# A token mixer's output product on Trainium2, rewritten from eight block products into seven products of quarters

## The chip, the cores and the metric

The kernel runs on one core of one Trainium2 chip. The metric is device time in microseconds (us) of one execution. The kernel before took 2018.16, 2018.16 and 2019.1 us in three runs: the median is 2018.16 us.

## What is computed

A decoder trunk of two layers over 512 tokens of width 1024, in float32. Each layer is a SwiGLU half-step, a token mixer and a second SwiGLU half-step, with a LayerNorm after each:

```python
x = layer_norm(ALPHA * x + 0.5 * swiglu(x, ffn1_w13[l], ffn1_w2[l]), ln_g[l, 0], ln_b[l, 0])
m = mixer(x, w_in[l], ..., w_branch_a[l], w_branch_b[l], w_out[l])
x = layer_norm(ALPHA * x + m, ln_g[l, 1], ln_b[l, 1])
x = layer_norm(ALPHA * x + 0.5 * swiglu(x, ffn2_w13[l], ffn2_w2[l]), ln_g[l, 2], ln_b[l, 2])
```

The end of the mixer is what matters here:

```python
y_a = o @ w_branch_a                                  # heads of the recurrence, 512 x 512
y_b = (u * mixed.reshape(B, T, SG_WIDTH)) @ w_branch_b
y = jax.nn.sigmoid(za) * y_a + jax.nn.sigmoid(zb) * y_b    # 512 tokens x 1024
return y @ w_out                                      # 1024 x 1024
```

## The kernel before, in words

**Products.** A float32 operand is split into two fp32r parts, hi and lo: `split` (L126 on ScalarE copies the source into hi, L127 on VectorE writes source minus hi into lo). One product is then three matmuls (hi hi, hi lo, lo hi) that add up in PSUM. Weights come over SyncE's queue into a ring of four raw buffers (`raw`, NRAW = 4), and their parts go to a ring of ten (`w`, NW = 10). The eight PSUM banks go round as one ring too.

**Seven products.** Most products of the kernel are made with seven products of quarter matrices in the place of eight, with sums and differences of quarters as operands (the table P1 to P7). The class `Seven` does this for the second products of the SwiGLUs, 11 pairs of 128-wide blocks each. Its method `sums_in_dram` forms the weight sums t1 to t4 with copying and accumulating DMAs on GpSimd's (POOL's) queue, in DRAM, long ahead of use. `activation_sums` forms s1 and s2 on VectorE (s3, s4 take the place of quarters of the activations) and splits s1 and s2; `later` splits the rest. `two_b`, `two_c` and `two_d` load and split the weights. `run` issues the products: P1, P6, P5 into the banks pA, pB, pC, then P2 and P3 into pA and pC, which end token rows 0 and 1 (128 tokens each), then P7 into pB and P4 into pF, which end rows 2 and 3. `add_to` (L202) adds a bank of 128 x 512 into the rows of the residual stream x on VectorE. `norm` works off the LayerNorm of a row: nm on VectorE (L215), the squares on ScalarE (L218), rstd on GpSimd (L186, L187), two steps in place on VectorE (L229, L230); its rows are then handed to a side task, `to_features`.

**The end of the mixer.** For each of eight 128-wide column blocks d of y, two projections of 12 matmuls each (`proj`, L155) make the branches' part, VectorE multiplies them by the gates z and adds the two (L1338, L1340), and the sum is split into yt. Two neighbouring blocks d, d + 1 share a load of the branch weights. `out_proj` then takes the product with w_out as eight blocks: the first three blocks k for all four token rows, the others row by row, so that the rows end one after the other, each followed by its norm. Weight loads, splits and matmuls stand in the order in which the code writes them, on each engine. The only things set in by time are the side tasks of `Flow`: a generator waits until an estimated clock (216 ns for a matmul) has passed its due time, then takes a step at one of the ticks that follow each group of three matmuls. So `to_features`, started by the norm with a delay, puts the transposes of a row (L176), and the splits of the transposed x (xh, xl; four tiles of 256 features, two token rows to each half) between the matmuls around it.

**Beyond it.** `first_weights` is called within the output product: it loads and splits the weights a and b of the next SwiGLU's first two blocks. That SwiGLU begins with them on the first 256 tokens (pa, pb; L155; 256-wide matmuls), which need the transposed rows 0 and 1, and later the other 256 tokens; then follow its pairs of blocks with seven products (fX, fA, fC; L661). Other pieces of the mixer that the prediction names: the recurrence's heads, whose outputs need rs, worked out by GpSimd (L186, L187), and `ln_params` (L192, L193), which loads the LayerNorm's factors over GpSimd's queue.

## Time and profile before

| | |
|---|---|
| runs | 2018.16, 2018.16, 2019.1 us; median 2018.16 |
| the profiled execution | 2016.08 us, of which its span (first to last instruction) 2014.3 |
| TensorE (PE) busy | 2003.1 us, 99% of the span, 13600 matmul records |
| TensorE's weight load (PEld) | 1863.7 us, 93% |
| VectorE (DVE) | 1659.4 us, 82% |
| ScalarE (ACT) | 1055.2 us, 52% |
| GpSimd (POOL) | 364.6 us, 18% |
| HBM | read 401.35 MB, written 147.85 MB: 273 GB/s over the span |

The profile follows one execution; its engines' names stand above in brackets, SP is SyncE, whose only work here is to issue DMAs. A row of a view names a line of the kernel, the engine, the operation, the tiles (out<-in) with their shape, and its times; "x4" are four instructions in one row. In a row of a timeline the first number is the start from the span's start and the second the time that the row lasted. "[1.36 <-ACT sq L218]" says that the engine stood idle 1.36 us before it, released by that instruction. A name ending in q ("POOLq", "SPq") is an engine's queue of DMAs; the last number of such a row is the median time from issue to landing.

### The profile page before, as it was taken

The numbers are of one execution on the slowest core, as the hardware profiler recorded it, in microseconds if no ns is written. First come the engines' busy times: TensorE is split into PE (matmuls) and PEld (weight loads), VectorE is DVE, ScalarE is ACT, GpSimd is POOL, SyncE is SP. The second block draws the span as 40 slices with busy tenths as digits, with TensorE's granted clock in tenths as the row PEclk, the third lists the DMA queues.
The fourth block names the chain that finished last, engine by engine and source line by source line (L and its number), as shares of the span: only waits on it lengthen the run. The fifth ranks groups of instructions, "written<-read, shape, count | busy, mean of one in ns | idle before, by whom it ended". The sixth has DMA issues, their size and how long they took to land.

```text
span 2014.3 us, 34802 instructions
## 1 busy us (share of the span) xinstructions
PE 2003.1 (99%) x13600; PEld 1863.7 (93%) x13600; DVE 1659.4 (82%) x2443; ACT 1055.2 (52%) x1545; POOL 364.6 (18%) x493
## 2 busy tenths in 40 slices
PE   9999999999999999999999999999999999999998
PEld 8999988998998999998899999888989989999986
DVE  8888888977766798889789889889778657988986
ACT  5545665336543455556555456652465435454563
POOL 0322002311000133210122320032110001332101
PEclk9999999999999999999999999999999999999999
DMA  6999776885343289987649997778853533999773
GB/s 240 271 266 235 250 261 225 198 228 185 102 169 115 105 231 264 255 229 265 207 148 284 266 244 261 250 235 208 211 164 96 180 112 110 259 257 243 247 252 125
DMA packets 173060, 425.67 MB, mean 211 GB/s; under 512 B 19264, under 2 KB 19392, under 8 KB 172896
## 3 DMA queue, kind: packets, MB, share of 16 engines
q1 hardware_dynamic: 114624, 265.41, 38.9%
q0 software_dynamic: 58272, 158.04, 32.5%
q8 instruction: 107, 1.75, 0.3%
q14 instruction: 57, 0.47, 0.1%
HBM read 401.35 MB, written 147.85 MB: 273 GB/s over the span
## 4 chain that ended last, share of the span: by engine, by line
PE 99%; DVE 0%; issue 0%; ACT 0%; DVEq 0%; ACTq 0%
PE fX L661 22%; PE fC L661 11%; PE pA L414 6%; PE pB L414 6%; PE pC L414 6%; PE cX L992 6%; PE fA L661 6%; PE y L290 4%; PE y L155 4%; PE pF L414 3%; PE cC L992 3%; PE f L155 2%; PE q L155 2%; PE iX L414 2%; PE g L155 2%; PE pa L155 2%
## 5 line engine op out<-in xcount | busy, mean ns | idle before, releaser
L126 ACT ACTIVATE h_pa<-ra 128x1024 fp32r<-128x1024 f32 x80 | 84.5, 1056 | 191.3 <-DVE ra L641 185.3
L355 POOL DMA_DIRECT2D t<-in_w_dram x176 | 145.8, 905 | 207.8 <-DMA t<-in_w_dram 115.6
L127 DVE TENSOR_TENSOR l_pc<-rc,h_pc 128x1024 fp32r<-128x1024 f32 x80 | 97.8, 1222 | 49.6 <-ACT h_pc L126 49.6
L355 POOL DMA_DIRECT2D t<-t x104 | 56.8, 547 | 287.8 <-DMA t<-in_w_dram 260.0
L127 DVE TENSOR_TENSOR l_pa<-ra,h_pa 128x1024 fp32r<-128x1024 f32 x80 | 97.7, 1222 | 2.5 <-ACT h_pa L126 2.4
L127 DVE TENSOR_TENSOR l_b<-r_b,h_b 128x1024 fp32r<-128x1024 f32 (+1 forms) x61 | 73.4, 1204 | 23.0 <-ACT h_b L126 22.3
L186 POOL TENSOR_SCALAR rstd<-ssq 128x1 f32<-128x1 f32 x23 | 18.5, 806 | 398.7 <-ACT sq L218 398.7
L661 PE MATMUL fX<-xh,l_pa 128*128 128x256 f32 x320 | 90.6, 283 | 0.0
L661 PE MATMUL fA<-xh,h_pc 128*128 128x256 f32 x320 | 90.6, 283 | 0.0
L661 PE MATMUL fA<-xl,h_pc 128*128 128x256 f32 x320 | 90.6, 283 | 0.0
L661 PE MATMUL fA<-xh,l_pc 128*128 128x256 f32 x320 | 90.6, 283 | 0.0
L661 PE MATMUL fC<-xs1h,h_pt 128*128 128x256 f32 x320 | 90.6, 283 | 0.0
L661 PE MATMUL fC<-xs1l,h_pt 128*128 128x256 f32 x320 | 90.6, 283 | 0.0
L661 PE MATMUL fC<-xs1h,l_pt 128*128 128x256 f32 x320 | 90.6, 283 | 0.0
L661 PE MATMUL fX<-xs2h,h_pa 128*128 128x256 f32 x320 | 90.6, 283 | 0.0
L661 PE MATMUL fX<-xs2l,h_pa 128*128 128x256 f32 x320 | 90.6, 283 | 0.0
L661 PE MATMUL fX<-xs2h,l_pa 128*128 128x256 f32 x320 | 90.6, 283 | 0.0
L661 PE MATMUL fC<-xs4h,h_pd 128*128 128x256 f32 x320 | 90.6, 283 | 0.0
L661 PE MATMUL fC<-xs4l,h_pd 128*128 128x256 f32 x320 | 90.6, 283 | 0.0
L661 PE MATMUL fC<-xs4h,l_pd 128*128 128x256 f32 x320 | 90.6, 283 | 0.0
L661 PE MATMUL fX<-xs3h,h_pb 128*128 128x256 f32 x320 | 90.6, 283 | 0.0
L661 PE MATMUL fX<-xs3l,h_pb 128*128 128x256 f32 x320 | 90.6, 283 | 0.0
(488 smaller groups left out, 7919.1 us busy)
## 6 DMA issues: line engine op xcount, KB each, us to landing
t<-in_w_dram POOLq DMA_DIRECT2D x88, 512.0 KB, 9.9
t<-t POOLq DMA_DIRECT2D x104, 256.0 KB, 4.8
t<-in_w_dram POOLq DMA_DIRECT2D x88, 256.0 KB, 7.1
r_c<-in_w_dram SPq DMA_DIRECT2D x44, 512.0 KB, 4.7
r_d<-t SPq DMA_DIRECT2D x88, 256.0 KB, 4.0
ra<-in_w_dram SPq DMA_DIRECT2D x80, 256.0 KB, 6.1
rb<-in_w_dram SPq DMA_DIRECT2D x80, 256.0 KB, 8.0
rc<-in_w_dram SPq DMA_DIRECT2D x80, 256.0 KB, 8.4
```

The costliest lines, as they stand in the source:

```text
L126: pin(S.activation(hi, src, AF.Copy))
L127: pin(V.tensor_tensor(lo, src, hi.bitcast(F32), op=ALU.subtract))
L155: PE.matmul(ps[:, n0:n0 + n], a[:, cs], m[:, n0:n0 + n], start=(i == 0), stop=(i == 3 * nk - 1))
L186: G.tensor_scalar(r, ssq, inv, eps, op0=ALU.mult, op1=ALU.add)
L290: PE.matmul(ys[t][q], a[:, ts], m[:, q * 512:(q + 1) * 512], start=(k == 0 and i == 0), stop=(k == nk - 1 and i == 2))
L355: tc.keep_in_program_order(nc.gpsimd.dma_start(*of(k), **kw))
L414: PE.matmul(ps[tt], a[:, ts], m, start=(start and k == self.order[0] and z == 0), stop=(stop and k == self.order[-1] and z == 2), skip_gro ...
L661: PE.matmul(ps[:, half[z]], a[:, ms], v, start=start, stop=(m == 3 and i == 2), skip_group_check=not (first and z == 0))
L992: PE.matmul(ps[:, half[z]], a[:, ms], v, start=first and z == 0 and m == 0 and i == 0, stop=(m == 3 and i == 2), skip_group_check=not (fir ...
```

## The change

The mixer's product with w_out goes through `Seven` in place of `out_proj`, which is gone. K is 8 blocks, so there are four pairs (k, k + 4); `run` and `sums_in_dram` get the few branches that so short a product wants (`few`, `early_d`). Each mixer makes its own weight sums with 24 DMAs on GpSimd's queue: a side task, started after the v projections, issues four at a time, 12000 ns of the estimated clock apart. The y blocks are made in the order of the pairs, d and d + 4 after one another, straight into the room of the quarters, and the activation sums of the pair follow at once. The arrays of the weights w_br and w_out are laid out anew by the host ahead of the run. In `run`, the steps `later(left.pop(0), 0)` and `later(k, 2)` change places, for the SwiGLUs too.

```diff
@@ -276,41 +276,6 @@
...
-    def out_proj(nk, lhs, w_of, c, ln, tag, first_weights):
...
-        tail = NW // 2
-        for k in range(nk):
-            w[k] = weights(w_of(k), f"{tag}{k}")
-            if k < nk - tail:
-                for t in range(NT):
-                    unit(k, t, (0, 1))
-        g, b = ln_params(*ln)
-        xs = load_rows()
-        begin_features()
-        for t in range(NT):
-            if t == 2:
-                first = first_weights()
-            sums = small("sums", 2)
-            for q in range(2):
-                for k in range(nk - tail, nk):
-                    unit(k, t, (q,))
-                add_to(xs[t], q, c, ys[t][q], sums)
-            norm(t, xs[t], sums, g, b, False, 9500.0)
-        return first
@@ -330,16 +295,16 @@
...
-        def __init__(self, w_of, order, spilled):
+        def __init__(self, w_of, order, spilled, tag="t"):
...
-        def sums_in_dram(self, pairs, group=3):
+        def sums_in_dram(self, pairs, group=3, gap=SUM_GAP):
@@ -353,7 +318,7 @@
                     for of, kw in ((copy, {}), (add, {"accum_op": ALU.add})):
                         for k in ks:
                             tc.keep_in_program_order(nc.gpsimd.dma_start(*of(k), **kw))
-                        yield 0.0, SUM_GAP
+                        yield 0.0, gap
         def part(self, k, a):
@@ -460,6 +425,7 @@
             A, B, C = ([bank(f"{v}{tt}") for tt in range(2)] for v in ("pA", "pB", "pC"))
+            few = self.n < NH2
             tail = 2
             fetched = {}
             left = list(ks)
@@ -475,14 +441,17 @@
                     fetched[v] = self.fetched(v)
                 h1, l1, h2, l2 = fetched[k]
                 ops["A11", k], ops["s1", k], ops["s2", k] = (h1, l1), (h2[:, 0], l2[:, 0]), (h2[:, 1], l2[:, 1])
-                if i < NH2 - tail:
+                if i < self.n - tail:
                     for ps, p in ((A, P1), (B, P6), (C, P5)):
                         for tt in range(2):
                             mm(ps, p, [k], tt, True, True)
-                if i >= LATER:
+                if few:
+                    if i:
+                        later(left.pop(0), 0)
+                elif i >= LATER:
                     for _ in range(min(2, len(left) - LATEST)):
                         later(left.pop(0), 0)
-                if i == LATER:
+                if i == (0 if few else LATER):
                     xs = load_rows()
             u = wk.tile([P, 2, 512], F32, tag="rs", name="u", bufs=2)
             for ps, p in ((A, P1), (B, P6), (C, P5)):
@@ -498,18 +467,20 @@
             tail = 2
             for i, k in enumerate(ks):
                 self.two_c(k)
-                if i < NH2 - LATEST:
+                if left and (few or i in (2, 3, 6)):
+                    later(left.pop(0), 0)
+                if few or i < NH2 - LATEST:
                     later(k, 2)
-                if left and i in (2, 3, 6):
-                    later(left.pop(0), 0)
-                if i in (4, 5):
-                    add_to(xs[i - 4], 1, -c, B[i - 4])
-                if 0 < i < NH2 - tail:
+                at = i - (1 if few else 4)
+                if at in (0, 1):
+                    add_to(xs[at], 1, -c, B[at])
+                if 0 < i < self.n - tail:
                     for ps, p in ((A, P2), (C, P3)):
                         for tt in range(2):
                             mm(ps, p, ks[0:2] if i == 1 else [k], tt, False, True)
             g, b = ln_params(*ln)
-            for k in ks[0:4]:
+            early_d = 2 if few else 4
+            for k in ks[0:early_d]:
                 self.two_d(k, True)
             if not last:
                 begin_features()
@@ -523,11 +494,11 @@
             F = [bank(f"pF{tt}") for tt in range(2)]
             tail = NW // 2
             for i, k in enumerate(ks):
-                if i in range(1, LATEST + 1):
+                if not few and i in range(1, LATEST + 1):
                     later(ks[i - LATEST - 1], 2)
-                if i >= 4:
+                if i >= early_d:
                     self.two_d(k)
-                if i < NH2 - tail:
+                if i < self.n - tail:
                     for ps, p in ((B, P7), (F, P4)):
                         for tt in range(2):
                             mm(ps, p, [k], tt, ps is F, True)
@@ -1274,6 +1245,8 @@
         flow.finish(in_dram)
         two_tokens()
         late.append(flow.add(all_out(), 4000.0))
+        so = Seven(lambda k: w_out[l, k], list(range(KT // 2)), [], "o")
+        out_sums = flow.add(so.sums_in_dram(so.order, 4, 12000.0), 8000.0)
         moments = []
         for t in range(NT):
             v = vt[t // 2][:, t % 2, :]
@@ -1324,24 +1297,23 @@
         s.clear()
         for t in late:
             flow.finish(t)
-        ys = []
         wbr = [None, None]
-        for d in range(KT):
-            yt = slot(f"yt{d}", F32R)
-            zs = []
-            for br, src in enumerate((ogs, sg)):
-                if d % 2 == 0:
-                    wbr[br] = weights(w_br[l, br, d // 2], f"br{br}{d}")
-                ps = bank(f"y{br}{d}")
-                proj(ps, wbr[br], (d % 2) * 512, lambda k: (src[k][:, 0, :], src[k][:, 1, :]), NH)
-                zv = z[br][d // 2][:, d % 2, :]
-                V.tensor_tensor(zv, zv, ps, op=ALU.mult)
-                zs.append(zv)
-            V.tensor_tensor(zs[0], zs[0], zs[1], op=ALU.add)
-            split(yt[:, 0, :], yt[:, 1, :], zs[0])
-            ys.append(yt)
-        return out_proj(KT, lambda k: (ys[k][:, 0, :], ys[k][:, 1, :]), lambda k: w_out[l, k], 1.0 / ALPHA, (l, 1),
-                        "wo", next_weights)
+        for k in range(4):
+            for a in range(2):
+                d = k + 4 * a
+                zs = []
+                for br, src in enumerate((ogs, sg)):
+                    if a == 0:
+                        wbr[br] = weights(w_br[l, br, k], f"br{br}{k}")
+                    ps = bank(f"y{br}{d}")
+                    proj(ps, wbr[br], a * 512, lambda h: (src[h][:, 0, :], src[h][:, 1, :]), NH)
+                    zv = z[br][d // 2][:, d % 2, :]
+                    V.tensor_tensor(zv, zv, ps, op=ALU.mult)
+                    zs.append(zv.rearrange("p (h t) -> p h t", h=2))
+                V.tensor_tensor(so.part(k, a), zs[0], zs[1], op=ALU.add)
+            so.activation_sums(k)
+        flow.finish(out_sums)
+        return so.run(1.0 / ALPHA, (l, 1), False, [], next_weights)
     lb = const.tile([P, DEPTH, NH], F32, name="lb")
     om = const.tile([P, DEPTH, NH], F32, name="om")
@@ -1455,12 +1427,12 @@
...
-    br = np.stack([np.asarray(v) for v in (w_branch_a, w_branch_b)], 1).reshape(DEPTH, 2, NH, P, 4, 2, P)
+    br = np.stack([np.asarray(v) for v in (w_branch_a, w_branch_b)], 1).reshape(DEPTH, 2, NH, P, 2, 4, P)
...
-        "w_br": c(br.transpose(0, 1, 4, 3, 5, 2, 6)).reshape(DEPTH, 2, 4, P, D),
-        "w_out": c(w_out).reshape(DEPTH, KT, P, D), "ln_g": c(ln_g), "ln_b": c(ln_b),
+        "w_br": c(br.transpose(0, 1, 5, 3, 4, 2, 6)).reshape(DEPTH, 2, 4, P, D),
+        "w_out": quarters(np.asarray(w_out), KT // 2), "ln_g": c(ln_g), "ln_b": c(ln_b),
```

VectorE's order, layer 0, at the end of the output product and around the hand-over to the SwiGLU. Names: y20 and y21 are the banks of the two halves of row 2, x1 and x2 rows of the stream, tr00 and tr01 hold the transposed row 0, tr10 and tr11 row 1, xh and xl are their parts. Before:

```order
L230 SCALAR_TENSOR_TENSOR x1_6851<-x1_6851,rstd_6954,lnb_6846 128x512 x2
L127 TENSOR_TENSOR xl0_6858<-tr00_7003,xh0_6857 128x2x128
L202 SCALAR_TENSOR_TENSOR x2_6853,sums_6987<-y20_6721,x2_6853 128x512
L127 TENSOR_TENSOR xl1_6860<-tr00_7003,xh1_6859 128x2x128
L127 TENSOR_TENSOR xl2_6862<-tr01_7018,xh2_6861 128x2x128
L202 SCALAR_TENSOR_TENSOR x2_6853,sums_6987<-y21_6722,x2_6853 128x512
L127 TENSOR_TENSOR xl3_6864<-tr01_7018,xh3_6863 128x2x128
L215 TENSOR_SCALAR nm_7042<-sums_6987 128x1
L229 SCALAR_TENSOR_TENSOR x2_6853<-x2_6853,nm_7042,lng_6845 128x512 x2
L230 SCALAR_TENSOR_TENSOR x2_6853<-x2_6853,rstd_7047,lnb_6846 128x512 x2
L127 TENSOR_TENSOR xl0_6858<-tr10_7069,xh0_6857 128x2x128
L127 TENSOR_TENSOR xl2_6862<-tr11_7083,xh2_6861 128x2x128
```

After, from the end of row 1's norm; a21 and b21 are weights of the SwiGLU's block 21, the second that it takes, pB0, pF0 the banks of row 2 and pB1, pF1 those of row 3:

```order
L230 SCALAR_TENSOR_TENSOR x1_6812<-x1_6812,rstd_7061,lnb_6981 128x512 x2
L127 TENSOR_TENSOR l_a21_7101<-r_a21_7098,h_a21_7100 128x1024
L127 TENSOR_TENSOR l_b21_7107<-r_b21_7104,h_b21_7106 128x1024
L202 SCALAR_TENSOR_TENSOR x2_6814,sums_7012<-pB0_6775,x2_6814 128x512
L202 SCALAR_TENSOR_TENSOR x2_6814<-pB0_6775,x2_6814 128x512
L202 SCALAR_TENSOR_TENSOR x3_6816,sums_7013<-pB1_6776,x3_6816 128x512
L202 SCALAR_TENSOR_TENSOR x2_6814,sums_7012<-pF0_7070,x2_6814 128x512
L202 SCALAR_TENSOR_TENSOR x3_6816<-pB1_6776,x3_6816 128x512
L215 TENSOR_SCALAR nm_7137<-sums_7012 128x1
L127 TENSOR_TENSOR xl0_6999<-tr00_7171,xh0_6998 128x2x128
L202 SCALAR_TENSOR_TENSOR x3_6816,sums_7013<-pF1_7071,x3_6816 128x512
L127 TENSOR_TENSOR xl0_6999<-tr10_7246,xh0_6998 128x2x128
```

Before, the splits of the transposed rows 0 and 1 stood among the additions and norms of the rows behind them: xl0 of row 0 right behind the norm of row 1, xl0 of row 1 (from tr10) right behind that of row 2. Now the norm's last step of row 1 is followed by two weight splits, all additions of rows 2 and 3 and the start of row 2's norm, with xl0 of row 0 behind nm and xl0 of row 1 behind the last addition of row 3.

TensorE's order at the same place: the output product's end, and the first matmuls of the SwiGLU (pa10 and pb10, the two parts of block 10, the first that it takes). Before:

```order
L290 MATMUL y31_6724<-h_wo7_6841,yt7_6685 128x512
L290 MATMUL y31_6724<-l_wo7_6842,yt7_6685 128x512
L290 MATMUL y31_6724<-h_wo7_6841,yt7_6685 128x512
L155 MATMUL pa10_7153<-xh0_6857,h_a10_6965 128x256
L155 MATMUL pa10_7153<-xl0_6858,h_a10_6965 128x256
L155 MATMUL pa10_7153<-xh0_6857,l_a10_6966 128x256
L155 MATMUL pa10_7153<-xh0_6857,h_a10_6965 128x256
L155 MATMUL pa10_7153<-xl0_6858,h_a10_6965 128x256
```

After:

```order
L176 MATMUL tr01_7185<-ident_67,x0_6810 128x128 x4
L379 MATMUL pF1_7071<-h_d3_7082,s33_6977 128x512
L379 MATMUL pF1_7071<-l_d3_7083,s33_6977 128x512
L379 MATMUL pF1_7071<-h_d3_7082,s33_6977 128x512
L176 MATMUL tr10_7246<-ident_67,x1_6812 128x128 x4
L176 MATMUL tr11_7257<-ident_67,x1_6812 128x128 x4
L155 MATMUL pa10_7242<-xh0_6998,h_a10_7088 128x256
L155 MATMUL pb10_7243<-xh0_6998,h_b10_7094 128x256
L155 MATMUL pa10_7242<-xl0_6999,h_a10_7088 128x256
L155 MATMUL pa10_7242<-xh0_6998,l_a10_7089 128x256
L155 MATMUL pa10_7242<-xh0_6998,h_a10_7088 128x256
L155 MATMUL pa10_7242<-xl0_6999,h_a10_7088 128x256
```

Before, the pa matmuls began behind the last y with the transposes of rows 0 and 1 done long ago, and ran on to 21 of them before the transposes of row 2. Now the transposes tr01 and tr10, tr11 stand among and right behind the last three matmuls of pF1, and pa and pb alternate behind them.

GpSimd's order in layer 0, where the heads' rs are formed. Before, only these stood here, and the LayerNorm's factors (lng) came next:

```order
L186 TENSOR_SCALAR rs_5878<-ms_5876 128x4
L187 TENSOR_TENSOR rs_5878<-rs_5878,mhalf_68 128x4
L186 TENSOR_SCALAR rs_5896<-ms_5894 128x4
L187 TENSOR_TENSOR rs_5896<-rs_5896,mhalf_68 128x4
L192 DMA lng_6845<-in_ln_g_dram 128x1024
```

After (o13, o2 and o4 are the sums in DRAM):

```order
L320 DMA o130_5257<-in_w_out_dram 256x1x512
L320 DMA o131_5258<-in_w_out_dram 256x1x512
L320 DMA o132_5259<-in_w_out_dram 256x1x512
L320 DMA o133_5260<-in_w_out_dram 256x1x512
L320 DMA o20_5261<-o130_5257 128x512
L320 DMA o20_5261<-o131_5258 128x512
L320 DMA o22_5262<-o132_5259 128x512
L320 DMA o22_5262<-o133_5260 128x512
L186 TENSOR_SCALAR rs_5900<-ms_5898 128x4
L187 TENSOR_TENSOR rs_5900<-rs_5900,mhalf_68 128x4
L186 TENSOR_SCALAR rs_5918<-ms_5916 128x4
L187 TENSOR_TENSOR rs_5918<-rs_5918,mhalf_68 128x4
```

Four accumulating and four copying DMAs stand ahead of these rs, and eight further DMAs behind them.

More of the change, by code (lines that the diff above doesn't have):

```diff
@@ L277, in need @@
                 ready[t] = None
-    def out_proj(nk, lhs, w_of, c, ln, tag, first_weights):
-        ys = [[bank(f"y{t}{q}") for q in range(2)] for t in range(NT)]
-        w = {}
-        def unit(k, t, qs):
-            hi, lo = w[k]
-            lh, ll = lhs(k)
-            ts = slice(t * P, (t + 1) * P)
-            for i, (a, m) in enumerate(((lh, hi), (lh, lo), (ll, hi))):
-                for q in qs:
-                    PE.matmul(ys[t][q], a[:, ts], m[:, q * 512:(q + 1) * 512],
-                              start=(k == 0 and i == 0), stop=(k == nk - 1 and i == 2))
-            flow.tick(3 * MM * len(qs))
-        tail = NW // 2
-        for k in range(nk):
-            w[k] = weights(w_of(k), f"{tag}{k}")
-            if k < nk - tail:
-                for t in range(NT):
-                    unit(k, t, (0, 1))
-        g, b = ln_params(*ln)
-        xs = load_rows()
-        begin_features()
-        for t in range(NT):
-            if t == 2:
-                first = first_weights()
-            sums = small("sums", 2)
-            for q in range(2):
-                for k in range(nk - tail, nk):
-                    unit(k, t, (q,))
-                add_to(xs[t], q, c, ys[t][q], sums)
-            norm(t, xs[t], sums, g, b, False, 9500.0)
-        return first
     def load_rows():
@@ L337, in __init__ @@
             self.r, self.t, self.last = {}, {}, None
-            self.t13 = [dram.tile([P, 2, 512], F32, name=f"t13{k}", tag=f"t13{k}", bufs=1) for k in range(n)]
-            self.t2 = [dram.tile([P, 2, 512], F32, name=f"t2{k}", tag=f"t2{k}", bufs=1) for k in range(0, n, 2)]
-            self.t4 = [dram.tile([P, 512], F32, name=f"t4{k}", tag=f"t4{k}", bufs=1) for k in range(n)]
-        def sums_in_dram(self, pairs, group=3):
+            self.t13 = [dram.tile([P, 2, 512], F32, name=f"{tag}13{k}", tag=f"{tag}13{k}", bufs=1) for k in range(n)]
+            self.t2 = [dram.tile([P, 2, 512], F32, name=f"{tag}2{k}", tag=f"{tag}2{k}", bufs=1) for k in range(0, n, 2)]
+            self.t4 = [dram.tile([P, 512], F32, name=f"{tag}4{k}", tag=f"{tag}4{k}", bufs=1) for k in range(n)]
+        def sums_in_dram(self, pairs, group=3, gap=SUM_GAP):
             for at in range(0, len(pairs), group):
```

## Prediction

> **What bounds the kernel now.** I read the page first: busy times, then the chain that ended last.
>
> ```profile
> span 2014.3 us, 34802 instructions
> PE 2003.1 (99%) x13600; PEld 1863.7 (93%) x13600; DVE 1659.4 (82%) x2443; ACT 1055.2 (52%) x1545; POOL 364.6 (18%) x493
> PE 99%; DVE 0%; issue 0%; ACT 0%; DVEq 0%; ACTq 0%
> ```
>
> The span is TensorE's own work. Nothing else is late anywhere, so a matmul taken away is worth its whole time, unless what was hidden beside it comes out. I therefore cut the windows view at the edges of the stage that changes, in layer 0: the output product (627 to 672.5), then the second SwiGLU's first blocks up to its first product of pairs (697.5).
>
> ```profile
> 627.30:640.00 12.70, 12.70 (x57) 10.52 (x57) 6.42 (x7) 5.83 (x6) 0.00 (x0) 1.00 0.52 165
> 640.00:660.00 20.00, 20.00 (x90) 16.54 (x90) 11.16 (x20) 5.56 (x7) 2.53 (x4) 1.00 0.33 107
> 660.00:672.50 12.50, 12.50 (x65) 10.40 (x64) 8.83 (x20) 4.85 (x13) 4.18 (x6) 1.00 0.15 51
> 672.50:685.00 12.50, 12.50 (x106) 12.46 (x105) 6.76 (x16) 6.15 (x18) 2.52 (x4) 1.00 0.93 327
> 685.00:697.50 12.50, 12.50 (x107) 12.50 (x106) 11.77 (x19) 9.12 (x16) 0.00 (x0) 1.00 0.01 2
> ```
>
> Columns: window, its length, then busy time of PE, PEld, DVE, ACT, POOL, granted clock, DMA share, GB/s. PE fills every window; VectorE (DVE) has 26.4 of 45.2 us in the product and 44.9 of 70.2 in all. So VectorE has 25 us to spare in this stretch, and any gain must live within them. TensorE's timeline gives the fixed points.
>
> ```profile
> 627.34 0.62 PE L290 MATMUL y<-h_wo,yt 128*128 128x512 f32 x2
> 628.25 1.07 PE L290 MATMUL y<-h_wo,yt 128*128 128x512 f32 x4
> 629.61 1.07 PE L290 MATMUL y<-h_wo,yt 128*128 128x512 f32 x4
> 672.70 0.28 PE L155 MATMUL pa<-xh,h_a 128*128 128x256 f32 x1
> 672.82 0.28 PE L155 MATMUL pa<-xl,h_a 128*128 128x256 f32 x1
> 675.25 0.60 PE L176 MATMUL tr<-ident,x 128*128 128x128 f32 x4
> 697.50 0.28 PE L661 MATMUL fX<-xh,h_pa 128*128 128x256 f32 x1
> ```
>
> Six 512-wide matmuls start between 628.25 and 629.61: 0.2267 us each; a 256-wide one takes 0.12. I count time from the product's first matmul: T = 627.34. The SwiGLU's first matmul stands at T+45.36, its products at T+70.16.
>
> **The change part by part.** *Matmuls.* 8 x 4 x 2 x 3 = 192 become 7 products x 4 x 2 x 3 = 168 of the same shape: 24 x 0.2267 = 5.44 us less per mixer, 10.9 in two. TensorE could be at the SwiGLU at T+39.9.
>
> *VectorE.* The quarters need 14 weight splits of 1024 columns where 8 served (six more), sums and splits of the activations, six more additions into the rows, two into pB. All stand in one in-order queue. Durations come from the same code at the end of the first SwiGLU, and from the norm of this stage:
>
> ```profile
> 301.00 1.89 DVE L127 TENSOR_TENSOR s<-r,s 128x512 fp32r<-128x512 f32 x3
> 302.80 2.35 DVE L127 TENSOR_TENSOR l_d<-r_d,h_d 128x1024 fp32r<-128x1024 f32 x2
> 305.07 0.68 DVE L202 SCALAR_TENSOR_TENSOR x<-pA,x 128x512 f32<-128x512 f32 x1
> 305.68 0.69 DVE L202 SCALAR_TENSOR_TENSOR x<-pC,x 128x512 f32<-128x512 f32 x1
> 309.91 1.41 DVE L229 SCALAR_TENSOR_TENSOR x<-x,nm,lng 128x512 f32<-128x512 f32 x2
> 311.24 1.41 DVE L230 SCALAR_TENSOR_TENSOR x<-x,rstd,lnb 128x512 f32<-128x512 f32 x2
> ...
> 662.94 0.42 DVE L127 TENSOR_TENSOR xl<-tr,xh 128x256 fp32r<-128x256 f32 x1
> 663.28 0.68 DVE L202 SCALAR_TENSOR_TENSOR x<-y,x 128x512 f32<-128x512 f32 x1
> 674.40 0.21 DVE L215 TENSOR_SCALAR nm<-sums 128x1 f32<-128x1 f32 x1
> 675.97 1.42 DVE L229 SCALAR_TENSOR_TENSOR x<-x,nm,lng 128x512 f32<-128x512 f32 x2 [1.36 <-ACT sq L218]
> 677.85 1.42 DVE L230 SCALAR_TENSOR_TENSOR x<-x,rstd,lnb 128x512 f32<-128x512 f32 x2 [0.46 <-POOL rstd L187]
> 679.19 0.75 DVE L127 TENSOR_TENSOR xl<-tr,xh 128x256 fp32r<-128x256 f32 x2
> ```
>
> From start to start: 1.135 us for 1024 columns, 0.605 for 512, 0.665 for one half of a norm's step, 0.34 for 256; a norm takes 4.8 us from nm to its end. Now the order of the changed kernel. The SwiGLU's first matmul with xl0 needs xl0 of token rows 0 and 1, and the second of these splits stands on VectorE behind everything that the product asks for. From T up to it there are 27 rows of 512, 14 of 1024, 8 norm halves, 6 of 256 and three nm: 16.3 + 15.9 + 5.3 + 2.0 + 0.5 = 40.0 us, without one pause.
>
> Pauses there will be. For them I need ScalarE's split and the loads:
>
> ```profile
> 632.53 1.06 ACT L126 ACTIVATE h_wo<-r_wo 128x1024 fp32r<-128x1024 f32 x1 [2.90 <-PE y L290]
> r_d<-t SPq DMA_DIRECT2D x88, 256.0 KB, 4.0
> ra<-in_w_dram SPq DMA_DIRECT2D x80, 256.0 KB, 6.1
> ```
>
> The buffer of h_c0 is read until matmul 30 (30 x 0.2267 = 6.8 us); with 1.06 of ScalarE, l_c0 starts at T+7.9, when VectorE has been free since about 6.1: 1.8 us. Waits of the first norm (square and rstd, 1.36 and 0.46 in the rows, half of the first under other work): 1.2. The last y, 0.2; dependent steps of the activation sums and the buffer of h_c1, about 0.8. Together 4.0, with bounds of 1.5 (only the first, nearly) and 5.5 (every norm wait in full, late splits beside it). So xl0 is ready at T+44.0 where TensorE comes at 39.9: **it waits 4.1**. The next steps repeat this on a small scale. The nm of row 2 stands 1.4 ahead, so x2 is normalized at 44.0 - 1.4 + 4.8 = 47.4; TensorE has 14 matmuls (1.7 us) before its transposes: 1.7 more. The xl1 splits stand behind this norm: 0.4. The last xl2 split stands among the steps of row 3's norm, at about 53.9, TensorE is there at 53.1: 0.8. Sum 7.0 us, between 4.5 and 8.5 by the pauses. After it VectorE no longer holds TensorE: before, row 3's norm ended at 679.19 and its transposes came 4 us later.
>
> Per mixer 7.0 - 5.44 = +1.56; for two **+3.1 us**, between -1.9 and +6.1.
>
> *ScalarE* gets the same splits at about 0.97 each and has 31.5 of 70.2 us busy: hidden. *w_br and w_out* are laid out anew outside the measured program: nothing. *y in pairs d, d + 4*: the same 16 projections; per pair VectorE gains about 1.1 us of sums and loses none; the y stage has 14.05 of 20.3 busy (607 to 627.3; the windows view again, below), so TensorE's order there is untouched.
>
> ```profile
> 607.00:627.30 20.30, 20.30 (x91) 16.84 (x90) 14.05 (x19) 5.72 (x7) 0.00 (x0) 1.00 0.29 97
> ```
>
> *Weight sums in DRAM.* 24 DMAs per mixer on POOL's queue, behind the pow of rstd and ahead of the heads' rs. Nearest rows are the SwiGLU's sums and the rs rows of this stage:
>
> ```profile
> L355 POOL DMA_DIRECT2D t<-in_w_dram x176 | 145.8, 905 | 207.8 <-DMA t<-in_w_dram 115.6
> ...
> t<-in_w_dram POOLq DMA_DIRECT2D x88, 512.0 KB, 9.9
> ...
> 514.27 1.01 POOL L187 TENSOR_TENSOR rs<-rs,mhalf 128x4 f32<-128x4 f32 x1
> 533.40 0.20 POOL L186 TENSOR_SCALAR rs<-ms 128x4 f32<-128x4 f32 x1 [18.12 <-DVE ms L1207]
> 577.67 0.61 POOL L192 DMA_DIRECT2D lng<-in_ln_g_dram  x1 [34.95 <-PE cX L992]
> ```
>
> The four accumulating DMAs issue from 515.3 (0.905 each), the last lands near 528.8; the four copies behind them wait for that, POOL is free at about 531, and rs wants it at 533.4. Slack 2.4 us; then two more such rounds, done near 571, before lng at 577.7. Price nothing; if a landing slips, the wait goes to VectorE's next instruction, which needs rs. SP gets 14 more loads: no wait.
>
> *A rule on the clock.* When TensorE ends, its granted clock does not stay:
>
> ```profile
> 2004.78 0.39 PE L414 MATMUL pF<-h_d,s 128*128 128x512 f32 x1
> 2006.50:2007.00 0.50, 0.00 (x0) 0.00 (x0) 0.35 (x4) 0.32 (x2) 0.00 (x0) 1.00 0.00 0
> 2007.00:2007.50 0.50, 0.00 (x0) 0.00 (x0) 0.50 (x2) 0.00 (x0) 0.41 (x1) 0.71 0.00 0
> ```
>
> It falls about 2 us after the last matmul has ended. The 4.1 us wait is broken by single matmuls only, so the clock may fall there, and it is a rival below. The Trainium skill (TensorE: Matmul & The Clock Gate, "Why this matters for your kernels") says to leave no idle gap over about 3 us between bursts; the trace agrees that idling costs the clock, but shows no gap inside the program. By that page's window of 3.4 us at half speed the sum would be up to 1.7 us per mixer higher, +6.5 in all.
>
> **The rivals.** *Late loads (slower).* The raw ring has four buffers, so r_d2 is loaded only when l_c2 is done, at T+18.6: its second half lands at 18.6 + 0.4 + 4.0 = 23.0, h_d2 is ready at 24.1, and VectorE comes to l_d2 at 24.4. Only 0.3 is spare, and everything behind it shifts one for one. At the 6.1 us of the ra rows it is 1.8 later per mixer: +6.7, 2024.9. It decides from about 4.8 us. For: three queues load there. Against: the stage's DMA share is 0.15 to 0.52.
>
> *The full gain.* If rows 0 and 1 came through in time, -10.9: 2007.3. For: VectorE's 25 us to spare. Against: they are not where they are needed; 40.0 of pure work stand ahead of xl0.
>
> *The clock falls.* Two to four us of matmuls at half speed while TensorE is the late one: 1 to 2 per mixer, 2023.3 to 2025.3. Against: VectorE is late then, and slow matmuls hide in the later waits of 2.9 us.
>
> *POOL late.* Sums that land 3 to 5 us late hold rs and VectorE's queue: up to +2.5 per mixer, 2026.
>
> *It doesn't do what it says:* the order shows 48 PE rows fewer. Ruled out.
>
> **How the numbers follow.** The profiled execution took 2016.08 for its span of 2014.3; +3.1 gives 2019.2. The median of the runs is 2018.16, so **2021.3**. About 0.2% (4.04 us) is what a measurement of this kernel can tell from no change. The forecast has 0.66: 0.50 of it within 0.2%, 0.16 above (from +4.04 to +6.1); late loads 0.10, the clock 0.07 and POOL 0.05, all slower; the full gain 0.12. That gives faster 0.12, same 0.50, slower 0.38. The range takes the forecast's bounds, 2016.2 to 2024.3, and reaches to the loads and the clock, 2025.3; the full gain is left out.
>
> **What would show it.** Right: 168 matmuls in 38 us without a pause; then TensorE idle 3 to 5 us before the first pa and pb, released by the additions into x2 and by xl0; about 1.5 before row 2's transposes; fX near T+71.7 in both layers, not 70.2. VectorE near 63 of some 72 us busy. Wrong: no idle time there (full gain), waits for h_d2 on a DMA, a granted clock under 1.00 in the window, or an idle PE at the heads' outputs.

## The result and the profile after

The changed kernel takes 2032.95 us (median of four runs, 2031.64 to 2033.1) where the kernel before takes 2018.58 (2018.16 to 2019.1): 14.4 us more. The ratio is 1.007, with a 95% interval of 1.0052 to 1.0087. The forecast was 2021.3 in a range up to 2025.3: the direction was right, the size and the main cause were not. The profiled execution took 2032.86 us for its span of 2031.1.

First the changed kernel's page, its busy times, and the view of what TensorE waited for (us in total, times, longest). Line numbers are those of the changed kernel.

```profile
span 2031.1 us, 34958 instructions
PE 2002.8 (99%) x13552; PEld 1861.8 (92%) x13552; DVE 1701.1 (84%) x2519; ACT 1073.4 (53%) x1577; POOL 398.8 (20%) x541
```

```profile
PE cX L963 <- DVE z L1002: 8.9, 3, 4.1
PE pa L155 <- DVE xl L127: 3.2, 2, 1.6
PE pa L155 <- DVE x L202: 2.3, 2, 1.1
PE pb L155 <- DVE x L202: 1.5, 2, 0.8
```

TensorE's busy time is 0.3 us less than before, although 48 matmuls of 0.2267 us (10.9 us) are gone. So busy time has been added somewhere by slow matmuls, and some 16 us of waiting stand beside it. The largest wait isn't at the output product at all: it is in the gates (cX), the stage that works out the factors z of the branches, whose matmuls the change doesn't touch.

I then measured the stages between fixed points of TensorE's timeline, in both layers. The points are a matmul of the v and i projections (iX), the output product's first matmul (T), and the first product of pairs (fX).

| stage | before | after | difference |
|---|---|---|---|
| start to iX, layer 0 | 476.99 | 477.62 | +0.63 |
| iX to T, layer 0 (gates, y) | 150.35 | 158.54 | +8.19 |
| T to fX, layer 0 (output product, hand-over) | 70.16 | 71.96 | +1.80 |
| fX to T, layer 1 (SwiGLUs, mixer, gates, y) | 931.01 | 936.72 | +5.71 |
| T to fX, layer 1 | 70.15 | 71.92 | +1.77 |
| fX to the end | 315.64 | 314.34 | -1.30 |

The sum is 16.8 us, the difference of the two spans; the medians differ by 14.4, since the profiled execution of the kernel before was 2.5 us below its median. The last row isn't TensorE's: its last matmul ends 306.5 us behind fX in both. The end behind that is shorter where the sums are made (the kernel before with the sums alone, run e3_before_with_sums, has 314.34 too) and as before without them (e2_no_sums, 315.60); why, no run shows. The output product costs +1.8 per mixer where +1.56 was forecast. The gates cost 8.2 and 5.7, where nothing was forecast.

*The gates.* GpSimd's timeline of the changed kernel, layer 0, from the four accumulating DMAs to the fourth copy and the third rs:

```profile
515.88 4.35 POOL L320 DMA_DIRECT2D o<-in_w_out_dram  x4
524.24 0.57 POOL L320 DMA_DIRECT2D o<-o  x1 [4.01 <-DMA o<-in_w_out_dram]
528.90 0.54 POOL L320 DMA_DIRECT2D o<-o  x1 [4.09 <-DMA o<-in_w_out_dram]
534.47 0.52 POOL L320 DMA_DIRECT2D o<-o  x1 [5.03 <-DMA o<-in_w_out_dram]
538.48 0.52 POOL L320 DMA_DIRECT2D o<-o  x1 [3.48 <-DMA o<-in_w_out_dram]
539.07 0.19 POOL L186 TENSOR_SCALAR rs<-ms 128x4 f32<-128x4 f32 x1
```

The accumulating DMAs issue at 515.9, as worked out (515.3). But they land one by one, 4 to 5.6 us apart, and each of the four copies waits for its own: GpSimd is free at 539.0, not at 531. The rs that was formed at 533.4 before starts at 539.07. VectorE's and TensorE's timelines show what hangs on it (ms is VectorE's sum of squares from which GpSimd forms rs). First VectorE before the change, then VectorE and TensorE after it:

```profile
534.72 0.69 DVE L1210 TENSOR_TENSOR on<-o,rs 128x512 f32<-128x512 f32 x1 [1.41 <-POOL rs L187]
```

```profile
533.26 0.69 DVE L1178 TENSOR_REDUCE ms<-o 128x4 f32<-128x512 f32 x1 [0.18 <-ACT o L1176]
540.41 0.69 DVE L1181 TENSOR_TENSOR on<-o,rs 128x512 f32<-128x512 f32 x1 [6.47 <-POOL rs L187]
541.02 0.68 DVE L1002 TENSOR_TENSOR z<-z,cX 128x512 f32<-128x512 f32 x1
```

```profile
537.37 0.28 PE L963 MATMUL cC<-xs4h,l_zd 128*128 128x256 f32 x1
541.75 0.58 PE L963 MATMUL cX<-xh,h_zy 128*128 128x256 f32 x1 [4.11 <-DVE z L1002]
```

VectorE stands 6.47 us before the product with rs (1.41 before the change), the subtraction that frees the bank of cX stands behind that, and TensorE waits 4.11 us for it. Then comes a second loss. The windows view (columns as in the prediction; the granted clock is the third number from the end):

```profile
535.00:540.00 5.00, 2.64 (x23) 2.44 (x21) 0.00 (x0) 1.06 (x1) 1.37 (x3) 0.99 0.75 272
540.00:542.00 2.00, 0.25 (x1) 0.25 (x2) 1.59 (x3) 0.27 (x1) 0.38 (x1) 0.50 0.24 90
542.00:544.00 2.00, 2.00 (x10) 2.00 (x11) 2.00 (x3) 1.84 (x3) 0.00 (x0) 0.50 0.00 0
544.00:546.00 2.00, 2.00 (x12) 2.00 (x11) 1.79 (x2) 0.10 (x1) 0.00 (x0) 0.50 0.00 0
546.00:548.00 2.00, 2.00 (x16) 2.00 (x16) 0.11 (x1) 0.60 (x1) 0.00 (x0) 0.82 0.55 133
```

The clock falls to half in the wait and stays there for nearly 5 us of work (in windows of half a microsecond, from about 539.9 to 546.7): 10, 12 and 16 matmuls fall in windows of 2 us, against 19 at full clock (e4_filled_gap, below). In layer 1 the wait is 3.41 us. A third wait of 1.34 us stands in layer 0's next gate block, behind VectorE's step that waits 2.75 us for the load zh.

*The hand-over.* TensorE and VectorE of the changed kernel at the end of the output product, layer 0:

```profile
636.16 0.39 PE L379 MATMUL pA<-h_b,th 128*128 128x512 f32 x1
675.14 1.04 PE L176 MATMUL tr<-ident,x 128*128 128x128 f32 x8
677.32 0.35 PE L155 MATMUL pa<-xh,h_a 128*128 128x256 f32 x1 [1.14 <-DVE x L202]
678.45 0.38 PE L155 MATMUL pb<-xh,h_b 128*128 128x256 f32 x1 [0.77 <-DVE x L202]
680.44 0.58 PE L155 MATMUL pa<-xl,h_a 128*128 128x256 f32 x1 [1.61 <-DVE xl L127]
```

```profile
679.36 0.68 DVE L202 SCALAR_TENSOR_TENSOR x<-pF,x 128x512 f32<-128x512 f32 x1
679.97 0.42 DVE L127 TENSOR_TENSOR xl<-tr,xh 128x256 fp32r<-128x256 f32 x1
```

With T = 636.16, xl0 of row 1 is ready at T+44.2, and TensorE's matmul with it starts at T+44.3: the forecast said 44.0. TensorE was there at T+40.0 and stood still for 1.14 + 0.77 + 1.61 = 3.5 us, with two single matmuls between.

### The profile page after: what moved, and what is told of

It is laid out like the page before. It is cut to its first block, busy times and chain, and to the rows that moved or that the text cites. A ratio compares the mean times of both kernels' runs of the same rounds, so it can differ in the third digit from the quotient of the medians.

```text
span 2031.1 us, 34958 instructions
## 1 busy us (share of the span) xinstructions
PE 2002.8 (99%) x13552; PEld 1861.8 (92%) x13552; DVE 1701.1 (84%) x2519; ACT 1073.4 (53%) x1577; POOL 398.8 (20%) x541
## 5 line engine op out<-in xcount | busy, mean ns | idle before, releaser
L127 DVE TENSOR_TENSOR l_b<-r_b,h_b 128x1024 fp32r<-128x1024 f32 (+1 forms) x69 | 83.4, 1209 | 24.0 <-ACT h_b L126 23.3
L126 ACT ACTIVATE h_b<-r_b 128x1024 fp32r<-128x1024 f32 (+1 forms) x69 | 71.9, 1042 | 57.4 <-DMA r_b<-t 29.7
L127 DVE TENSOR_TENSOR l_c<-r_c,h_c 128x1024 fp32r<-128x1024 f32 x60 | 72.6, 1223 | 28.7 <-ACT h_c L126 28.1
```

The lines of the kernel that those rows point to most:

```text
L126: pin(S.activation(hi, src, AF.Copy))
L127: pin(V.tensor_tensor(lo, src, hi.bitcast(F32), op=ALU.subtract))
```

## The experiments

Theory A: the copies that wait for DMAs to land hold rs on GpSimd's queue, rs holds VectorE, VectorE holds TensorE, and the clock adds to it. Rival B: the DMAs' traffic delays the gates' loads. Rival C: something else in the change (the order of y, buffers) costs the gates. The kernel before ran beside each of them, on the same chip.

| run | us | before | ratio, 95% interval | iX to T, layer 0 | T to fX, layers 0 and 1 |
|---|---|---|---|---|---|
| e1_rs_first | 2019.21 | 2017.08 | 1.0012 (1.0003 to 1.0021) | 150.36 | 71.88, 71.97 |
| e2_no_sums | 2020.81 | 2017.08 | 1.0015 (1.0007 to 1.0024) | 150.36 | 71.52, 71.98 |
| e3_before_with_sums | 2030.19 | 2017.08 | 1.0065 (1.0053 to 1.0078) | 158.91 | 70.15, 70.14 |
| e4_filled_gap | 2029.14 | 2017.08 | 1.0058 (1.0045 to 1.0071) | 156.56 | 71.73, 71.56 |
| f1_s4_in_y_stage | 2016.38 | 2017.64 | 0.9993 (0.9984 to 1.0002) | | 70.68, 71.33 |
| f2_late_a21_b21 | 2018.93 | 2017.64 | 1.0006 (0.9997 to 1.0015) | | 72.28, 72.54 |
| f3_both | 2018.53 | 2017.64 | 1.0003 (0.9994 to 1.0012) | | 71.74, 72.02 |
| f4_lo_on_gpsimd | 2022.06 | 2017.64 | 1.0022 (1.0012 to 1.0031) | | 73.52, 74.23 |
| g1_filled_handover | 2019.12 | 2017.03 | 1.0009 (1.0 to 1.0018) | | 71.62, 72.05 |
| g2_filled_and_s4 | 2016.49 | 2017.03 | 0.9997 (0.9988 to 1.0006) | | 70.66, 70.60 |
| g3_filled_s4_s3 | 2015.36 | 2017.03 | 0.9994 (0.9985 to 1.0003) | | 70.18, 69.01 |
| g4_raw_ring_five | 2038.28 | 2017.03 | 1.0102 (1.0088 to 1.0116) | | 70.28, 70.48 |
| h1_s4_s3_in_y_stage | 2015.54 | 2016.84 | 0.9994 (0.9985 to 1.0003) | | 69.17, 70.81 |

**e1_rs_first.** The six steps of the sums get a list of gaps, so that the waiting copies come behind the last two rs:

```diff
...
-        out_sums = flow.add(so.sums_in_dram(so.order, 4, 12000.0), 8000.0)
+        out_sums = flow.add(so.sums_in_dram(so.order, 4, (12000.0, 30000.0, 8000.0, 8000.0, 8000.0)), 8000.0)
```

> Same 24 DMAs per mixer, but the four copies o2 <- o13, which wait for the accumulating DMAs to land, stand on GpSimd's queue behind the last two rs instead of ahead of them. Theory A (the wait for the landing holds rs, rs holds VectorE, VectorE holds TensorE, whose clock then halves): the gates lose at most 2 us per mixer instead of 8.2 and 5.4, so 2020 to 2023 us. Rival B (the DMAs' traffic itself delays the gates' weight loads): still 2030 or more. Under both the first fX stays some 72 us behind the output product's first matmul.

2019.21 us, 2.1 above the kernel before, and the gates take 150.36 us, as before the change. The same DMAs on GpSimd's timeline of this run:

```profile
515.19 4.35 POOL L321 DMA_DIRECT2D o<-in_w_out_dram  x4
533.35 0.20 POOL L186 TENSOR_SCALAR rs<-ms 128x4 f32<-128x4 f32 x1 [13.80 <-DVE ms L1180]
533.62 1.03 POOL L187 TENSOR_TENSOR rs<-rs,mhalf 128x4 f32<-128x4 f32 x1
541.37 0.19 POOL L186 TENSOR_SCALAR rs<-ms 128x4 f32<-128x4 f32 x1 [6.71 <-DVE ms L1180]
541.65 1.01 POOL L187 TENSOR_TENSOR rs<-rs,mhalf 128x4 f32<-128x4 f32 x1
542.61 2.19 POOL L321 DMA_DIRECT2D o<-o  x4
```

The third rs starts at 533.35 again, and the copies go out without a wait. The four accumulating DMAs run at the same time as in the changed kernel, and the gates lose nothing, so B falls as the main cause; theory A holds. In small, loads do take longer: the load zh behind the third wait landed 9.9 us after its issue in the changed kernel, beside the next round of sums, 6.8 in this run, and 4.0 before the change and in e2_no_sums. So that wait, 1.34 of the 8.19 us, may be B's.

**e2_no_sums.** The 24 DMAs of each mixer are left out, and the loads of t1 to t4 read w_out itself, so the output product is another one of the same size:

```diff
-        out_sums = flow.add(so.sums_in_dram(so.order, 4, 12000.0), 8000.0)
+        so.t13 = [w_out[l, k][:, 0:3:2] for k in so.order]
+        so.t2 = [w_out[l, k][:, 1:3] for k in (0, 2)]
+        so.t4 = [w_out[l, k][:, 3] for k in so.order]
...
```

> Leaves the 24 DMAs of each mixer out; the loads of t1 to t4 read w_out itself (so the output product is another one, of the same size). Theory A and rival B both: the gates are as before, 2018.6 + 2 x 1.8 = about 2022 us by the output product alone; if it stays near 2030, the loss in the gates has nothing to do with the sums.

2020.81 us, and 150.36 us for the gates: no faster than e1_rs_first. Once rs stands first, the DMAs cost nothing that this shows.

**e3_before_with_sums.** The kernel before, with the same side task; its results are read by nothing. w_out is laid out in quarters here too, which the sums need, and the old product reads its blocks from there:

```diff
...
         late.append(flow.add(all_out(), 4000.0))
+        so = Seven(lambda k: w_out[l, k], list(range(KT // 2)), [], "o")
+        out_sums = flow.add(so.sums_in_dram(so.order, 4, 12000.0), 8000.0)
...
```

> The kernel before, with the same 24 DMAs per mixer at the same place on GpSimd's queue, their results unused. Theory A and B: 2018.6 + 8.2 + 5.4 = about 2032 us although the product is the old one. Rival C (the gates lose through something else in the change, such as the order of y or buffers): 2018 to 2020 us.

2030.19 us, +13.1, with 158.9 us from iX to T: the old output product with the sums' queue loses what the new one loses in the gates (iX to T in layer 1 is 156.53, 155.88 in the changed kernel and 150.36 before). Its own stage, T to fX, is as before, so the new layout costs nothing there. C falls.

**e4_filled_gap.** Thirty useless matmuls where TensorE stands still, into a bank that is free there:

```diff
             product(C, "s4", d or load(ring("zd"), w[:, 2]), "zd", False)
+            if step == 1:
+                for _ in range(30):
+                    PE.matmul(A[:, lo_t], xh[0][:, 0, 0:P], xh[0][:, 0, lo_t], start=True, stop=True,
+                              skip_group_check=True)
```

> The changed kernel with 30 useless 256-wide matmuls (3.6 us) in each mixer in the second gate block, where TensorE stands still 4.1 and 3.4 us; they write a bank that is free there. Theory A with the clock: the idle time falls to 0.5 us or none, the clock stays at 1.00 and each mixer gains 1.5 to 2.5 us: 2028 to 2030 us, faster with more work. Rival D (the clock falls for another reason, or the slow matmuls hide in later waits): 2033 us or up to 0.5 us more.

2029.14 us. Against the kernel before this is +12.1, the changed kernel has +14.4: 60 more matmuls, 2.3 us less. The two intervals overlap, so the totals alone don't tell them apart; the stages do. TensorE's timeline and the windows of this run:

```profile
541.57 0.39 PE L963 MATMUL cX<-xh,h_zy 128*128 128x256 f32 x1 [0.38 <-DVE z L1002]
```

```profile
540.00:542.00 2.00, 1.62 (x13) 1.42 (x13) 1.77 (x3) 0.45 (x1) 0.20 (x1) 1.00 0.20 78
542.00:544.00 2.00, 2.00 (x19) 2.00 (x18) 2.00 (x3) 1.76 (x3) 0.00 (x0) 1.00 0.03 8
```

The matmul that VectorE releases starts at about the same time (541.57, not 541.75), but the clock is 1.00 and 19 matmuls fall in a window of 2 us where the changed kernel has 10. So about 2 of the gates' 8.2 us in layer 0 are the clock's (158.54 becomes 156.56), the rest is the waits. In layer 1 the same stage, iX to T, falls from 155.88 to 154.17, so 1.7 us there; fX to T falls by 0.7 only, but it holds two SwiGLUs as well. The expectation holds.

The next runs build on e1_rs_first and ask what holds back the product's own gain of 5.4 us per mixer.

**f1_s4_in_y_stage.**

```diff
...
             so.activation_sums(k)
+            if k in (0, 1, 2):
+                so.later(k, 0)
```

> Kernel of run e1_rs_first, with three of the eight splits of the activations' quarters (s4 of pairs 0, 1 and 2) made right behind their sums in the y stage, where VectorE has 3.6 of 20.2 us free, instead of in the output product: 3 x 0.605 = 1.8 us less on VectorE ahead of xl0. Theory (VectorE's in-order queue holds TensorE at the end of the product, and the clock halves in the wait): the waits of 1.3 + 0.8 + 1.6 us fall to about 1.9, the clock stays up or falls later, and the first fX comes 68 to 70.5 us behind the product's first matmul instead of 71.9: 2014 to 2017 us. Rival (the loads or the chain of additions and norms hold it, not the queue's length): 71.5 or more, 2018 to 2020 us.

T to fX shrinks by 1.2 and 0.6 us, less than the 1.8 taken from the queue: 70.7 and 71.3 lie between theory and rival. The time is 1.3 below the kernel before, which the interval doesn't tell from no change.

**f2_late_a21_b21** and **f3_both.** The subtractions of these two splits are kept in a list and made in `ffn`; f3 has the edits of f1 and f2:

```diff
...
             need(0, 1)
+            for hi, lo, raw in lows:
+                V.tensor_tensor(lo, raw, hi.bitcast(F32), op=ALU.subtract)
```

> Kernel of run e1_rs_first, with VectorE's part of the splits of the SwiGLU's weights a21 and b21 (2 x 1.135 = 2.3 us) taken out of the queue ahead of xl0 and put behind the transposed rows 0 and 1. Theory: the first waits fall by 2.3 us, but the work comes back before the product of pairs, so 69 to 71.5 us from the product's first matmul to the first fX and 2015 to 2018.5 us; the gain is smaller than the work moved if VectorE is full up to fX. Rival: no difference, 2018 to 2020 us.

> Both edits of the two runs before it. Theory: xl0 comes 4.1 us earlier, as early as TensorE wants it; 66.5 to 70 us to fX, clock at 1.00, 2010 to 2016 us, below the kernel before. Rival: no better than the better of the two.

Both theories fail and the rivals hold. The first waits do shrink (f2 waits 0.27 + 1.61 in layer 0), but fX comes 72.3 and 72.5 us behind the product's first matmul: waits for the norms of rows 2 and 3, for xh and for xl come up behind. Work that is only put off within this stretch is due again before fX. f3 is no better than f1.

**f4_lo_on_gpsimd.**

```diff
...
+                if self.n < NH2:
+                    S.activation(v[:, 0, :], src, AF.Copy)
+                    G.tensor_tensor(v[:, 1, :], src, v[:, 0, :].bitcast(F32), op=ALU.subtract)
+                else:
+                    split(v[:, 0, :], v[:, 1, :], src)
...
```

> Kernel of run e1_rs_first, with the lo parts of all eight quarters s3 and s4 of the output product made by GpSimd instead of VectorE: 8 x 0.605 = 4.8 us off VectorE's queue. Theory: if GpSimd takes under 2 us for one, xl0 is ready as TensorE comes and fX follows at 66 to 69 us: 2010 to 2015 us. Rival: GpSimd is slow or slows VectorE down, the product itself waits for s4 and s3, and the time is over 2019 us.

The rival holds: 73.5 and 74.2, 2022.06 us. Two of GpSimd's subtractions of this run, and two of VectorE's:

```profile
641.99 1.30 POOL L427 TENSOR_TENSOR s<-r,s 128x512 fp32r<-128x512 f32 x1
644.51 2.27 POOL L427 TENSOR_TENSOR s<-r,s 128x512 fp32r<-128x512 f32 x1
```

```profile
647.79 2.31 DVE L127 TENSOR_TENSOR l_d<-r_d,h_d 128x1024 fp32r<-128x1024 f32 x1
654.01 1.21 DVE L127 TENSOR_TENSOR l_d<-r_d,h_d 128x1024 fp32r<-128x1024 f32 x1
```

GpSimd needs 1.30 us for one, but 2.27 while VectorE makes a split of 1024 columns; such a split takes VectorE 2.31 us beside GpSimd and 1.21 once GpSimd is done.

**g1_filled_handover**, **g2_filled_and_s4**, **g3_filled_s4_s3** and **g4_raw_ring_five.** Useless matmuls in `proj`, behind the first matmul of pa and pb (6 and 13 times); g3 also calls `so.later(k, 2)` in the y stage, and g4 changes the buffer counts:

```diff
...
+                if fill and i == 0:
+                    to, times = fill
+                    for _ in range(times):
+                        PE.matmul(to[:, 256:512], a[:, cs], m[:, 0:256], start=True, stop=True, skip_group_check=True)
...
-    NS, NRAW, NSA = 34, 4, 3
+    NS, NRAW, NSA = 33, 5, 3
```

> Kernel of run e1_rs_first, with 19 useless 256-wide matmuls per mixer (6 behind the first of pa, 13 behind the first of pb, 2.3 us) in the waits at the end of the output product; they write a half of the banks that is begun anew later. Theory (the waits of 1.3 + 0.8 + 1.6 us, with two single matmuls among them, halve the clock for some 6 us, which costs about 3 us per mixer): the clock stays at 1.00, the first fX comes 68.5 to 69.5 us behind the product's first matmul instead of 71.9, and the time is 5 to 6.5 us below that of e1_rs_first, about 3 to 4.5 us below the kernel before. Rival (slow matmuls hide in the later waits for the norms of rows 2 and 3): no more than 1 us per mixer, about as before.

The rival holds. A window of e1_rs_first, then two of g1_filled_handover, at the hand-over of layer 0:

```profile
672.00:674.00 2.00, 2.00 (x10) 2.00 (x11) 1.54 (x3) 0.37 (x2) 1.62 (x2) 0.50 0.54 150
```

```profile
672.00:674.00 2.00, 1.94 (x16) 1.70 (x14) 1.82 (x5) 1.79 (x4) 0.59 (x1) 1.00 0.05 19
674.00:676.00 2.00, 1.00 (x8) 0.79 (x7) 1.54 (x4) 0.00 (x0) 1.09 (x2) 1.00 0.79 248
```

With the useless matmuls the clock stays at 1.00, but TensorE then waits 1.02 us for row 2's norm, and T to fX is 71.6 and 72.1 as without the filling. Here the halved clock costs nothing: VectorE is late, and the slow matmuls only fill the wait for it.

> The same useless matmuls in the kernel of run f1_s4_in_y_stage, whose first fX came 70.7 and 71.3 us behind the product's first matmul. Theory: 67.5 to 69 us, 3 to 5 us below the kernel before. Rival: no more than 1 us per mixer better than without them.

> As g2_filled_and_s4, with three splits of s3 made in the y stage too (1.8 us less on VectorE behind the product's first matmul). Theory: another 0.5 to 1.8 us per mixer unless the loads of r_d2 and r_d3, for which ScalarE waits, have become the limit. Rival (the loads hold it now): within 0.5 us of g2_filled_and_s4.

> As g3_filled_s4_s3, with five buffers in the raw ring in place of four and 33 slots in place of 34, so that r_d2 and r_d3 are loaded one split earlier. If the loads are the limit in g3, another 0.5 to 1.5 us per mixer; if not, the same time, or more where the missing slot holds something up.

g2 is as f1 in layer 0 and 0.7 better in layer 1: the filling brings little here too, not what theory said. g3 gains 0.5 and 1.6 over g2. g4 settles nothing about the loads: T to fX is no shorter than in g3, but the kernel with one slot less is 21 us above the kernel before, nearly all of it in other stages (TensorE waits 15.1 us in four places for fX's banks).

**h1_s4_s3_in_y_stage.** g3 without the useless matmuls.

> Kernel of run g3_filled_s4_s3 without the useless matmuls: sums in DRAM behind rs, and six of the eight splits of quarters in the y stage (3.6 us off VectorE's queue in the output product). Theory (VectorE's queue ahead of xl0 is what holds the product's gain back): the first fX comes 67.5 to 69.5 us behind the product's first matmul in place of 71.9 in e1_rs_first and 70.2 before, and the time is 2 to 5 us below the kernel before. Rival (the splits moved only shift the wait to another cover, the loads or the norms): 70 us or more, as f1_s4_in_y_stage.

69.2 and 70.8: in layer 0 within the theory's band, in layer 1 not. The clock tells the layers apart. Windows at about the same place behind the product's first matmul, layer 0, then layer 1:

```profile
674.00:676.00 2.00, 1.87 (x16) 1.80 (x16) 1.08 (x4) 2.00 (x7) 0.38 (x2) 1.00 0.80 209
```

```profile
1675.00:1677.00 2.00, 2.00 (x12) 2.00 (x11) 1.14 (x3) 1.95 (x5) 0.41 (x1) 0.50 0.97 310
```

TensorE waits about as long in both (1.40 + 1.02 and 1.61 + 0.83 us), but the clock stays at 1.00 in layer 0 and is 0.50 from 1672.5 to 1679.3 in layer 1. In g3_filled_s4_s3, whose clock stays at 1.00 in both, layer 1 has 69.01 (and layer 0, where the useless matmuls gain no clock, 70.18). So with less work on VectorE the half clock does cost at the hand-over, some 1.6 us by these single executions.

VectorE has 3.6 us less to do, and fX comes 2.7 and 1.2 us earlier than in e1_rs_first; new waits take part of it: 1.45 us for h_d, which waits for its load, and 0.85 for pB, which VectorE now reaches before TensorE is done. The time is 1.3 us below the kernel before, not the 2 to 5 of the theory and inside the uncertainty. No version was clearly faster than the kernel before.

## Why the prediction was wrong

**The step that failed is the one on the weight sums in DRAM:** "the last lands near 528.8; the four copies behind them wait for that, POOL is free at about 531 [...] Slack 2.4 us [...] Price nothing". It read the landing from a group's median (9.9 us) that mixes copying and accumulating DMAs, and set it behind the last issue. Here the four are all accumulating, beside the gates' loads, and the last copy could go only 18.3 us after the last issue ended (520.2 to 538.5). The trace of before had the same pattern, on GpSimd's timeline, for the sums of the v and i weights, and I didn't look for it:

```profile
349.60 4.33 POOL L355 DMA_DIRECT2D t<-in_w_iv_dram  x4
362.15 0.57 POOL L355 DMA_DIRECT2D t<-t  x1 [8.22 <-issue]
364.00 0.55 POOL L355 DMA_DIRECT2D t<-t  x1 [1.27 <-DMA t<-in_w_iv_dram]
366.66 0.53 POOL L355 DMA_DIRECT2D t<-t  x1 [2.10 <-DMA t<-in_w_iv_dram]
369.42 0.53 POOL L355 DMA_DIRECT2D t<-t  x1 [2.23 <-DMA t<-in_w_iv_dram]
```

Four issues and four copies hold GpSimd from 349.6 to 370.0, 20.4 us. Set at 515.3, that gives 535.7: past the 533.4 at which rs is wanted. The slack of 2.4 us was a lateness of 2.3 by the nearest row, and 5.1 in the run: VectorE's ms is done at 533.95, rs starts at 539.07. TensorE's idle time at the heads' outputs, the last of the prediction's signs of being wrong, is what showed.

**The rival "POOL late" was the right mechanism with the wrong price and chance.** It had +2.5 per mixer, 2026 in all, at a chance of 0.05, and the range stopped short of it at 2025.3; the stages gave 8.2 and 5.7, and e3_before_with_sums, by its median, 13.1 for the two. Two things were left out of its price. The chain rs, VectorE, cX passes the delay on to TensorE nearly whole (4.11 of 5.1 us), since VectorE's queue has the subtraction that frees the bank right behind. And the clock rival was set at the hand-over only, while the gates were the place where it cost: about 2 us in layer 0 and 1.7 in layer 1, by e4_filled_gap.

**The output product was right.** Its sum, +1.56 per mixer, stands against +1.80 and +1.77; e1_rs_first, which no longer has the gates' loss, is 2.1 us above its kernel before where 3.1 was forecast (the stage's 3.5 in both layers, less the 1.3 at the end). The steps: 168 matmuls without a pause up to T+40.0 (39.9); xl0 at T+44.2 (44.0); idle time 3.5 us (4.1). The later waits of 2.9 us came as 0 and 0.55, but with 6.8 us at half clock in their place (679.8 to 686.7 in layer 0); filling the gap (g1_filled_handover) brings these waits back and leaves the sum. That was the argument against the clock rival, and it held here, as long as VectorE was late; h1_s4_s3_in_y_stage shows where it ends. The Trainium skill (TensorE: Matmul & The Clock Gate, "Why this matters for your kernels") asks for no idle gap over about 3 us between bursts. The runs agree: gaps of 4.11 and 3.41 us halved the clock, for 6.8 and 3.4 us, and the one of 1.34 didn't. At the hand-over it fell too, though no single wait there is over 1.61 us: three of them, 3.5 us in all, have only single matmuls between.

**Late loads** didn't come at the product of the changed kernel: no wait of TensorE names a DMA there. They showed only when VectorE had less to do (1.45 us for h_d in h1). In the gates one load was late, as e1_rs_first tells.

**The order of y and the loads on SP's queue** cost nothing up to the output product, as forecast: iX to T is 150.36 in e1_rs_first and 150.35 before.

What stays open: which of the loads, norms and additions would be the next limit if VectorE were freed further. It wasn't settled, since the run meant for the loads (g4) fell to the missing slot. Nor is it shown why the clock fell in one layer of h1 and not in the other.

## What to carry to other kernels

A step that is put on an idle engine's queue costs nothing only if nothing that others want stands behind its waits: count the wait for landing, not the issue, and take it from a row of the same pattern (so many of the same kind, issued together), not from a group's median. Where TensorE is the bound, price a late wait as its idle time plus the matmuls at half clock behind it, unless another engine is late there anyway (g1 against h1). A stage that fills TensorE may leave a second engine without a gap just where the gain would have to come out; moving its work ahead of the stage shortened the stage here (f1, h1), putting it off within the stage didn't (f2), though no total moved clear of the noise.

## What the runs showed of the hardware that was not expected

- After the gap of 3.41 us in layer 1 the clock fell only when TensorE was at work again. The matmul behind the gap starts at 1552.70; half-microsecond windows of the changed kernel:

```profile
1552.50:1553.00 0.50, 0.30 (x2) 0.31 (x3) 0.50 (x2) 0.33 (x1) 0.00 (x0) 1.00 0.00 0
1553.00:1553.50 0.50, 0.50 (x6) 0.50 (x5) 0.50 (x1) 0.50 (x2) 0.00 (x0) 1.00 0.00 0
1553.50:1554.00 0.50, 0.50 (x5) 0.50 (x4) 0.50 (x2) 0.50 (x1) 0.00 (x0) 0.64 0.00 0
1554.00:1554.50 0.50, 0.50 (x5) 0.50 (x4) 0.50 (x2) 0.34 (x2) 0.00 (x0) 0.50 0.00 0
...
1557.00:1557.50 0.50, 0.50 (x7) 0.50 (x5) 0.00 (x0) 0.00 (x0) 0.00 (x0) 0.95 0.00 0
```

  The fall comes some 4.4 us behind the end of the last matmul ahead of the gap, with 0.9 us of work already done, and lasts about 3.4 us. In layer 0 it came 2.2 us behind that end, within the wait, and lasted 6.8. So a wait that has ended can still be paid for.
- A 128x1024 subtraction on VectorE takes 1.2 us alone and 2.3 us beside 128x512 subtractions on GpSimd, which go from 1.3 to 2.3 us themselves (f4_lo_on_gpsimd); the help cost more than it brought.
- Four accumulating DMAs of 512 KB issued together landed 4 to 5.6 us apart in the gates of layer 0; the four for the v and i weights, of the same size, let their copies go 1.8 to 2.8 us apart. The copies that wait for them hold GpSimd's queue.
- Loads beside the sums took longer: the load zh of the gates behind the third wait took 9.9 us to land, 4.0 before the change and in e2_no_sums.
